# Narrow gate projections, decay rows by way of DRAM, full-row compressed values, and an earlier start in a two-block kernel

## The chip, the cores and the metric

One core of a Trainium2 chip runs the whole program. The metric is the device time of one execution in microseconds (us); the time given for a kernel is the median of its runs.

## What is computed

Two blocks follow each other on 512 latent rows of width 1024; the first also carries 256 context rows. In float32, cut to what matters here:

```python
for l in range(2):                                    # first block
    h  = rms_norm(x, g) * (1 + scale) + shift         # (shift, scale, gate) = silu(c) @ w_mod + b_mod
    hc = rms_norm(xc, g) * (1 + scale_c) + shift_c
    a*, b*, bg, c*, gm = split(h @ w_in)              # bg: 16 gate columns; same for hc
    y_a = diff_attention(...)                         # 4 heads
    y_b = mlstm(bq, bk, bv, bg)                       # 4 heads, both directions, decay matrix
                                                      # exp(b_t - b_s + i_s - m_t), masked
    y_c = neighbourhood_attention(cq, ck, cv)         # 8 heads of 64
    x, xc = merge(y_a, y_b, y_c, gm)
x = hybrid_ab(x) ; x = ffn(x)                         # second block
x = nsa(x) ; x = ffn(x)                               # 16 heads: compressed, selected and window
                                                      # values, each with a gate: 48 gate columns
```

## The kernel before

The activations stand transposed in SBUF: a chunk of 128 features by 512 latent and 256 context columns, split into a high and a low part (`hh`, `hl`). A projection of 128 output features takes a slot of weights: SP loads it as `raw` (`raw`, L327), ScalarE (ACT) casts the high part `whi` (L319), VectorE subtracts to get `wlo` (L320), and TensorE adds three products for each chunk of 128 inputs: `hh` with `whi`, `hl` with `whi`, `hh` with `wlo` (`proj`, L345; `tm_step` with tokens as the stationary side, L402). The slots lie in a ring of four, raw weights in three buffers, so SP loads some slots ahead.

The tile framework's scheduler sets the order of the instructions on each engine from the program text and the dependencies. The one exception is `start`, whose TensorE, VectorE and ScalarE instructions stand in the order of the text (L644).

The stages that the change touches:
- `start` (L611): layer 0. Latent and context columns are loaded, squared and summed on DVE, added over partitions by matmuls with a column of ones (`rstd`, L547), and spread as rows R (`rows`, L554). h is x times R, times scale, plus shift (`make_h`, L563, splits it); the products with R are DVE and GpSimd (POOL) instructions of their own (L650 to L673). Between them stand the units of the modulation, products of c with `w_mod` (`mod_products`, L486), whose row goes through ACT (L488) and two transposes (L746). The first value projection of the attention, `av`, runs alongside (L402). It takes all six row chunks for each pair of inputs. Layer 1's start (L1329) multiplies by R on DVE in the same way.
- The mLSTM gates, in `gates`: a projection with 16 columns (L345 with 128 x 16 weights), six transposes (L990), and a chain of small operations on rows that ends in Q (L1054), 48 columns, one for each direction, chunk and head.
- `mlstm`, once for each head: for each direction and chunk a column of Q is spread over the columns of a tile by a transpose of its broadcast (L1099), four to a bank; DVE adds the mask MK into the tile D (L1101) and ACT takes the exponential.
- `branch_c`, the neighbourhood attention: for each pair of heads and block of 128 queries two score tiles; a step later (`na_step`) their probabilities are transposed (L746), and a step after that `na_values` multiplies them with V (L1263), 64 columns for each head of the pair.
- NSA: `nsa_gates` (48 columns, four transposes L1819); `compress` makes VC, the compressed values; for each unit (group, query block, pair of heads) the probabilities are transposed four at a time (L746) and the unit before it is multiplied with V (L1972, 128 x 64). `nsa_values` is a generator, taken one group at a time between the transposes. Its first matmul is the compressed part with 64 rows of VC (L1968).

## Time and profile before

| | us |
|---|---|
| three runs | 3149.46, 3148.14, 3148.11 |
| median | 3148.14 |
| the profiled execution, its own time | 3147.98 |
| its span | 3146.2 |
| TensorE busy (in the span) | 3078.2 (98%) |
| VectorE busy | 1797.7 (57%) |
| ScalarE busy | 1257.6 (40%) |
| GpSimd busy | 300.9 (10%) |

The span is what the hardware profiler saw from the first instruction to the last, in one execution. An engine's busy time is the sum of its instructions' durations with overlaps counted once. TensorE's matmuls are pipelined: the next one starts before the one before has ended, so what a matmul costs is the distance from its start to the next start.

### The profile page before, as it was taken

How to read it: one execution, taken by the hardware profiler on the slowest of the kernel's cores; microseconds unless marked ns; L12 is line 12 of the kernel's file. 1: busy time of each engine (PE TensorE's matmuls, PEld its weight loads, DVE VectorE, ACT ScalarE, POOL GpSimd, SP SyncE). 2: the span in 40 equal slices, each digit the busy share in tenths (PEclk: the TensorE clock that was granted, in tenths of full speed). 3: DMA queues.
4: the chain of work that ended last, by engine and by line, in shares of the span. 5: the costliest groups of instructions: out<-in, count | busy, mean ns of one | idle time of the engine just before them, and what ended most of it. 6: DMA issues, size and time to landing. Idle time of an engine off the chain costs nothing.

```text
span 3146.2 us, 43890 instructions
## 1 busy us (share of the span) xinstructions
PE 3078.2 (98%) x17322; PEld 2572.0 (82%) x17322; DVE 1797.7 (57%) x3477; ACT 1257.6 (40%) x2382; POOL 300.9 (10%) x284
## 2 busy tenths in 40 slices
PE   7999999999999999999999999999999999999998
PEld 5888788888888888788888877788888788788887
DVE  6776256735574577346455477754433688644433
ACT  4553244325432356234344444332322267632221
POOL 1000000000015000000000400101100022101100
PEclk9999999999999999999999999999999999999999
DMA  6113211332235211311332533233223310022322
GB/s 225 41 34 135 71 60 48 127 115 72 84 138 205 87 49 48 111 54 61 110 104 88 161 100 102 67 101 101 94 94 104 99 41 28 28 94 94 101 92 69
DMA packets 86894, 285.96 MB, mean 91 GB/s; under 512 B 10400, under 2 KB 15264, under 8 KB 86304
## 3 DMA queue, kind: packets, MB, share of 16 engines
q1 hardware_dynamic: 68832, 237.60, 22.6%
q0 software_dynamic: 7424, 28.32, 2.5%
q10 hardware_dynamic: 10432, 17.24, 1.8%
q8 instruction: 136, 2.23, 0.3%
q14 instruction: 70, 0.57, 0.1%
HBM read 268.44 MB, written 14.68 MB: 90 GB/s over the span
## 4 chain that ended last, share of the span: by engine, by line
PE 88%; DVE 7%; issue 2%; ACT 2%; POOL 1%; DMA 0%; ACTq 0%; DVEq 0%; POOLq 0%
PE pj L345 57%; PE s L345 10%; PE s L746 4%; PE s L402 3%; PE s L741 2%; PE pj L402 2%; PE s L742 2%; PE s L1263 1%; PE pj L1972 1%; PE s L878 1%; PE s L1119 1%; DVE kl L737 1%; PE s L1145 1%; PE s L1138 1%; DVE kl L736 1%
## 5 line engine op out<-in xcount | busy, mean ns | idle before, releaser
L345 PE MATMUL pj<-hl,whi 128*128 128x512 f32 (+3 forms) x2696 | 939.5, 367 | 0.3 <-DVE hl L332 0.2
L345 PE MATMUL pj<-hh,whi 128*128 128x512 f32 (+3 forms) x2696 | 936.4, 369 | 2.6 <-ACT hh L331 0.8
L345 PE MATMUL pj<-hh,wlo 128*128 128x512 f32 (+3 forms) x2696 | 938.2, 367 | 0.0
L319 ACT CAST whi<-raw 128x1024 fp32r<-128x1024 f32 (+2 forms) x391 | 405.4, 1038 | 1088.8 <-PE pj L345 841.0
L320 DVE TENSOR_TENSOR wlo<-raw,whi 128x1024 fp32r<-128x1024 f32 (+2 forms) x391 | 488.1, 1249 | 443.4 <-ACT whi L319 434.4
L345 PEld LDWEIGHTS pj<-hh,whi 128*128 128x128 f32 (+2 forms) x2696 | 483.6, 187 | 92.7 <-issue 3.0
L345 PEld LDWEIGHTS pj<-hl,whi 128*128 128x128 f32 (+2 forms) x2696 | 483.0, 187 | 85.0 <-issue 1.9
L345 PEld LDWEIGHTS pj<-hh,wlo 128*128 128x128 f32 (+2 forms) x2696 | 482.9, 187 | 84.3 <-issue 1.7
L345 PE MATMUL pj<-uh,whi 128*128 128x512 f32 (+1 forms) x374 | 141.0, 377 | 0.0
L345 PE MATMUL pj<-ul,whi 128*128 128x512 f32 (+1 forms) x374 | 140.8, 376 | 0.0
L345 PE MATMUL pj<-uh,wlo 128*128 128x512 f32 (+1 forms) x374 | 140.8, 376 | 0.0
L741 PE MATMUL s<-kh,q 128*128 128x256 f32 (+1 forms) x320 | 101.2, 334 | 8.7 <-ACT kh L735 3.3
L700 ACT ACTIVATE th<-pj 128x512 f32<-128x512 f32 x72 | 37.3, 521 | 162.0 <-PE pj L345 150.3
L1715 DVE TENSOR_TENSOR a<-a,pj 128x512 f32<-128x512 f32 x44 | 30.3, 688 | 121.5 <-PE pj L345 121.5
L345 PE MATMUL s<-yh,whi 128*128 128x512 f32 (+1 forms) x288 | 98.7, 357 | 0.0
L345 PE MATMUL s<-yh,wlo 128*128 128x512 f32 (+1 forms) x288 | 98.0, 354 | 0.0
L345 PE MATMUL s<-yl,whi 128*128 128x512 f32 (+1 forms) x288 | 97.8, 354 | 0.0
L1713 POOL TENSOR_TENSOR a<-a,R 128x512 f32<-128x512 f32 x44 | 56.9, 1292 | 409.6 <-DVE a L1712 409.6
L1709 DVE TENSOR_TENSOR a<-pj,R 128x512 f32<-128x512 f32 x44 | 30.4, 691 | 113.5 <-PE pj L345 113.5
L742 PE MATMUL s<-kl,q 128*128 128x256 f32 (+1 forms) x320 | 92.7, 315 | 0.0
L345 PE MATMUL s<-hl,whi 128*128 128x512 f32 (+1 forms) x288 | 89.5, 347 | 0.0
L345 PE MATMUL s<-hh,wlo 128*128 128x512 f32 (+1 forms) x288 | 88.1, 345 | 0.0
(493 smaller groups left out, 4991.4 us busy)
## 6 DMA issues: line engine op xcount, KB each, us to landing
raw<-in_w SPq DMA_DIRECT2D x392, 512.0 KB, 3.4
mraw<-in_w SPq DMA_DIRECT2D x30, 512.0 KB, 4.9
bias<-in_bias ACTq DMA_DIRECT2D x16, 768.0 KB, 4.8
contrib<-cb POOLq DMA_DIRECT2D x16, 384.0 KB, 3.2
ld<-contrib POOLq DMA_DIRECT2D x16, 384.0 KB, 4.0
raw<-in_w SPq DMA_DIRECT2D x16, 384.0 KB, 2.9
contrib<-cb POOLq DMA_DIRECT2D x16, 256.0 KB, 2.6
ld<-contrib POOLq DMA_DIRECT2D x16, 256.0 KB, 3.1
```

Of the source, the lines that this page charges most:

```text
L319: nc.scalar.copy(hi[:, :width], raw[:, :width])
L320: nc.vector.tensor_sub(lo[:, :width], raw[:, :width], hi[:, :width].bitcast(F32))
L345: self.mm = self.nc.tensor.matmul(ps, wt[:, off + k * mcols:off + (k + 1) * mcols], acts[k][which][:, r], start=first and i == 0, stop=las ...
L402: self.nc.tensor.matmul(ps[c], self.h[k][a][:, P * c:P * c + P], b[:, w], start=k == 0 and pi == 0, stop=k == KD - 1 and pi == 2)
L700: self.nc.scalar.activation(th[:, r], p_, AF.Tanh, scale=0.5)
L736: nc.vector.tensor_sub(kl[a, c], r[a, c], kh[a, c].bitcast(F32))
L737: nc.vector.tensor_sub(kl[b, c], r[a, c], kh[a, c].bitcast(F32))
L741: self.nc.tensor.matmul(out, q[:, qs], kh[:, ks], start=True, stop=False)
L742: self.nc.tensor.matmul(out, q[:, qs], kl[:, ks], start=False, stop=True)
L746: self.nc.tensor.transpose(out[:, P * i:P * i + P], b, self.tab["id"])
L878: nc.tensor.matmul(po, at[:, P * i:P * i + P], V[:, k0 + i, P * h:P * h + P], start=i == 0, stop=i == nb - 1)
L1713: nc.gpsimd.tensor_mul(a, a, self.R)
```

## The change

- `narrow` replaces `proj` for the gate projections: high and low weights stand side by side as 32 (or 96) stationary columns, and two matmuls for each chunk, with `hh` and with `hl`, replace three. The two halves of the result are added by a matmul with a table of two stacked identities, which also transposes.
- Q is transposed once a layer, copied, and written by SP to `qrows` in DRAM; for each head SP loads its rows, broadcast to all partitions, into D, and DVE adds the mask in place.
- The neighbourhood values are multiplied two blocks at a time, with six buffers for the transposed probabilities.
- VC is padded with zeros to all 128 rows, one version for each pair of heads; `nsa_values` goes out in one piece ahead of the next unit's transposes.
- `start`: squares are added in pairs and the four sums by the matmuls with ones; the values' first slot is loaded ahead of the context; chunks of latent rows are multiplied for the first pair of inputs before the context's norm; the product with R is folded into `make_h`. Layer 1's start folds it too. Modulation units come in another order, and silu(c) moves into `start`.
- Smaller tiles of `compress` move to other buffers; the NSA gates are multiplied with R after their transposition.

The diff, cut:

```diff
+    def narrow(self, key, n, outs):
...
+        nc = self.nc
+        raw = self.raw(key)[:, :KD * n].rearrange("p (k f) -> p k f", k=KD)
+        w = self.t(self.ring, [P, SLOT], F32R, "whi", self.NRING)[:, :2 * n * KD].rearrange("p (k f) -> p k f", k=KD)
+        nc.scalar.copy(w[:, :, :n], raw)
+        nc.vector.tensor_sub(w[:, :, n:], raw, w[:, :, :n].bitcast(F32))
+        for ps, r in outs:
+            for k in range(KD):
+                for part in range(2):
+                    nc.tensor.matmul(ps, w[:, k, :], self.h[k][part][:, r], start=k == 0 and part == 0, stop=k == KD - 1 and part == 1)
...
-    def make_h(self, l, xs, js, part=None):
+    def make_h(self, l, xs, js, R, part=None, first=None):
...
-                nc.scalar.activation(hi[:, r], t[:, r], AF.Identity, bias=sh, scale=sc)
-                nc.vector.tensor_scalar(t[:, r], t[:, r], sc, sh, ALU.mult, ALU.add)
-            c = part[0] if part else slice(0, TT)
-            nc.vector.tensor_sub(lo[:, c], t[:, c], hi[:, c].bitcast(F32))
+                nc.vector.scalar_tensor_tensor(t[:, r], t[:, r], sc, R[:, r] if R.shape[-1] >= TT else R, ALU.mult, ALU.mult)
+                nc.scalar.activation(hi[:, r], t[:, r], AF.Identity, bias=sh)
+            if first:
+                first()
+            for r in part or both:
+                sh = mod[:, j, both.index(r):both.index(r) + 1]
+                nc.vector.scalar_tensor_tensor(lo[:, r], t[:, r], sh, hi[:, r].bitcast(F32), ALU.add, ALU.subtract)
...
-            units = [load(0)]
+            units = [load(0), load(1)]
+            av = [self.raw(("av", 0, 0))]
...
-            units.append(load(1))
-            ssq = self.t(sp, [P, TT], F32, "ssq")
+            units.append(load(2))
+            av.append(self.raw(("av", 0, 1)))
...
-                squares(lat)
-                rl = stats(lat)
-                squares(ctx)
+                rl = sums(squares(lat, range(4)), lat)
+                silu()
                 fin = self.mod_products(units[0], self.s1)
-                rows(lat, rl)
-                nc.vector.tensor_mul(xs[0][:, lat], rs[:, lat], xs[0][:, lat])
+                self.rows(rs, rl, 4)
+                slot = self.slot_hi(("av", 0, 0), av[0])
+                nc.scalar.copy(R[:, lat], rs)
                 fin()
-                rc = stats(ctx)
-                self.make_h(0, xs, (0,), (lat,))
-                slot = self.slot(("av", 0, 0))
                 fin = self.mod_products(units[1], self.s1)
-                rows(ctx, rc)
-                nc.vector.tensor_mul(xs[1][:, lat], R[:, lat], xs[1][:, lat])
+                self.make_h(0, xs, (0,), rs, (lat,), first=lambda: self.slot_lo(("av", 0, 0), *slot))
+                slot = slot[1:]
+                ps = self.tm_banks(NTC, True)
+                parts = self.tm_step("av", 0, 0, ps, 4, slot)
+                sq = squares(ctx, (0,))
                 fin()
-                self.make_h(0, xs, (1,), (lat,))
+                next(parts)
+                next(parts)
+                self.make_h(0, xs, (1,), R, (lat,))
+                fin = self.mod_products(units[2], self.s1)
+                sq += squares(ctx, (1, 2, 3))
+                next(parts)
+                fin()
+                units = [load(3)]
+                next(parts)
+                rc = sums(sq, ctx)
+                self.make_h(0, xs, (2,), R, (lat,))
+                slot = self.slot_hi(("av", 0, 1), av[1])
+                rows = self.s1()[:, :CTX]
+                self.rows(rows, rc, 2)
+                fin = self.mod_products(units[0], self.s1)
                 for j in range(2):
-                    nc.vector.tensor_mul(xs[j][:, ctx], R[:, ctx], xs[j][:, ctx])
-                    self.make_h(0, xs, (j,), (ctx,))
-                ps = self.tm_banks(NTC, True)
-                for s in range(4):
+                    self.make_h(0, xs, (j,), rows, (ctx,))
+                slot = self.slot_lo(("av", 0, 1), *slot)
+                nc.scalar.copy(R[:, ctx], rows)
+                self.make_h(0, xs, (2,), R, (ctx,))
+                next(parts)
+                fin()
+                self.make_h(0, xs, (3,), R)
+                for _ in parts:
+                    pass
+                for s in range(1, 4):
                     j = 2 * s + 2
-                    parts = self.tm_step("av", 0, s, ps, 4 * (s == 0), slot)
+                    parts = self.tm_step("av", 0, s, ps, 0, slot)
                     if s < 3:
                         units = [load(j + i) for i in range(2)]
                         next(parts)
                         fin = self.mod_products(units[0], self.s1)
                         slot = self.slot(("av", 0, s + 1))
-                        for i in range(2):
-                            (nc.vector, nc.gpsimd)[i].tensor_mul(xs[j + i], R, xs[j + i])
...
-        slot = self.slot(("bg", l))
-        outs = [(self.pj(SEQ, 16), slice(0, SEQ)), (self.pj(CTX, 16), slice(SEQ, TT))]
-        self.proj(slot, self.h, outs, mcols=16)
-        gs = self.t(sp, [16, TT], F32, "gs")
+        add = self.load(sp, "sum16")[0:32]
+        outs = [(self.pj(SEQ, 32), slice(0, SEQ)), (self.pj(CTX, 32), slice(SEQ, TT))]
+        self.narrow(("bg", l), 16, outs)
+        gs = self.t(sp, [32, TT], F32, "gs")
         for ps, r in outs:
-            nc.scalar.activation(gs[:, r], ps, AF.Identity, bias=self.par(("gate_b", l))[0:16])
+            nc.scalar.activation(gs[:, r], ps, AF.Identity, bias=self.par(("gate_b", l))[0:32])
...
         for c in range(NTC):
-            nc.tensor.transpose(pt[:, 16 * c:16 * c + 16], gs[:, P * c:P * c + P], self.tab["id"][0:16, 0:16])
+            nc.tensor.matmul(pt[:, 16 * c:16 * c + 16], gs[:, P * c:P * c + P], add, start=True, stop=True)
...
+        pq = self.s1()
+        nc.tensor.transpose(pq[0:48, :P], Q.rearrange("p d a h -> p (d a h)"), self.tab["id"])
+        qr = self.t(sp, [48, P], F32, "qr")
+        nc.vector.tensor_copy(qr, pq[0:48, :P])
+        nc.sync.dma_start(self.qrows[l], qr)
...
         D = [self.t(sp, [P, NTC, P], F32, f"D{d}", 1) for d in range(2)]
+        rows = qrows.rearrange("(d a h) t -> h d a t", d=2, a=6)
+        for d in range(2):
+            nc.sync.dma_start(D[d][:, :n, :], rows[h, d, :n].partition_broadcast(P))
         parts = []
         for cs in groups:
             parts.append([D[d][:, cs[0]:cs[-1] + 1, :] for d in range(2)])
             for d in range(2):
-                pe = self.s1()
-                for i, c in enumerate(cs):
-                    nc.tensor.transpose(ch(pe, i), Q[:, d, c, h:h + 1].to_broadcast([P, P]), self.tab["id"])
                 m = len(cs)
-                nc.vector.tensor_add(parts[-1][d], three(pe, m), MK[:, d, None, :].to_broadcast([P, m, P]))
+                nc.vector.tensor_add(parts[-1][d], parts[-1][d], MK[:, d, None, :].to_broadcast([P, m, P]))
...
-            pT = self.t(sp, [P, 512], F32, "pT", 4)
+            pT = self.t(sp, [P, 512], F32, "pT", 6)
             nc.scalar.copy(pT[:, :w], tp[:, :w])
             pTs.append(pT)
-        if ready:
-            self.na_values(*ready)
-        return pTs, *rest
-
-    def na_values(self, pTs, V, vt, out):
-
-        for x, j in enumerate(vt):
-            for i, pT in enumerate(pTs):
-                rows = slice(64 * i, 64 * i + 64)
-                self.nc.tensor.matmul(out[rows, :], V[:, j, rows], pT[:, P * x:P * x + P], start=x == 0, stop=x == len(vt) - 1)
+        if len(ready) == 2:
+            self.na_values(ready)
+        ready.append((pTs, *rest))
+
+    def na_values(self, ready):
+
+        for pTs, V, vt, out in ready:
+            for x, j in enumerate(vt):
+                for i, pT in enumerate(pTs):
+                    rows = slice(64 * i, 64 * i + 64)
+                    self.nc.tensor.matmul(out[rows, :], V[:, j, rows], pT[:, P * x:P * x + P], start=x == 0, stop=x == len(vt) - 1)
+        ready.clear()
...
-        VC = self.t(cp, [P, 4, P], F32, "VC")
+        VC = self.t(cp, [P, 2, 4, P], F32, "VC")
...
-            nc.vector.tensor_copy(VC[32 * x:32 * x + 32, :, r:r + 64], pt[0:32, :256].rearrange("p (g d) -> p g d", g=4))
+            nc.vector.tensor_copy(VC[32 * x:32 * x + 32, x // 2, :, r:r + 64], pt[0:32, :256].rearrange("p (g d) -> p g d", g=4))
...
             pr, cT, g, i, x, V, VC, y = unit
             blocks = [(k, r, j) for k in range(2) for j in range(i + 1) for r in range(2)]
             out = []
-        values = self.nsa_values(*ready) if ready else iter(())
+        if ready:
+            self.nsa_values(*ready)
         for b0 in range(0, len(blocks), 4):
             four = blocks[b0:b0 + 4]
...
-            next(values, None)
-        for _ in values:
-            pass
...
-        rows = slice(64 * x, 64 * x + 64)
         qs = slice(P * i, P * i + P)
-        nc.tensor.matmul(po, VC[rows, g, :], cT[rows, qs], start=True, stop=False)
+        nc.tensor.matmul(po, VC[:, x, g, :], cT[:, qs], start=True, stop=False)
...
-            if n == last:
-                nc.scalar.copy(y[:, qs], po)
-            yield
+        nc.scalar.copy(y[:, qs], po)
```

TensorE in the NSA stage, before: from a unit's window scores (L741, L742, with the parts `kwinh` and `kwinl` of the keys) over transposes (L746, with the identity `tab_id`) and values (L1968 compressed, L1972).

```order
L741 MATMUL s_3993_22565<-kwinh_21658,q_3822_21761 128x512
L742 MATMUL s_3993_22565<-kwinl_21659,q_3822_21761 128x512
L746 MATMUL s_3998_22584<-tab_id_77,pr_22441 128x128 x4
L1968 MATMUL pj_22591<-pcT_22130,VC_21326 128x128
L1972 MATMUL pj_22591<-pT_22482,V_21410 64x128 x4
L746 MATMUL s_4001_22597<-tab_id_77,pr_22441 128x128 x2
L746 MATMUL s_4001_22597<-tab_id_77,pr_22442 128x128 x2
L1972 MATMUL pj_22591<-pT_22495,V_21410 64x128 x4
L746 MATMUL s_4003_22608<-tab_id_77,pr_22442 128x128 x4
L1972 MATMUL pj_22591<-pT_22507,V_21410 64x128 x4
L741 MATMUL s_4009_22630<-kslch_21606,q_3844_21865 128x512
```

The same place with the change, where the scores are L799 and L800, transposes L804, the compressed values L2038 and the values L2042.

```order
L799 MATMUL s_3972_22456<-kwinh_21549,q_3801_21652 128x512
L800 MATMUL s_3972_22456<-kwinl_21550,q_3801_21652 128x512
L2038 MATMUL pj_22475<-pcT_22021,VC_21223 128x128
L2042 MATMUL pj_22475<-pT_22384,V_21301 64x128 x4
L2042 MATMUL pj_22475<-pT_22391,V_21301 64x128 x4
L2042 MATMUL pj_22475<-pT_22398,V_21301 64x128 x4
L804 MATMUL s_3978_22490<-tab_id_77,pr_22332 128x128 x4
L804 MATMUL s_3980_22497<-tab_id_77,pr_22332 128x128 x2
L804 MATMUL s_3980_22497<-tab_id_77,pr_22333 128x128 x2
L804 MATMUL s_3982_22504<-tab_id_77,pr_22333 128x128 x4
L799 MATMUL s_3988_22521<-kslch_21497,q_3823_21756 128x512
```

The values of a unit, which stood in three groups between the transposes, stand in one row of twelve ahead of them, behind the scores.

VectorE with the change, at the end of head 0 of layer 0's mLSTM: the outputs `hb` of head 0 (L1219, L1221), the additions of the mask to head 1's D (L1165), head 0's normalisation (L810, L812) and the next low weights (L328).

```order
L1221 SCALAR_TENSOR_TENSOR hb_3800<-nu_3993,dn_4001,hb_3800 128x128 x2
L1215 RECIPROCAL dn_4019<-dn_4019 128x2
L1165 TENSOR_TENSOR D_746_4317<-D_746_4317,MK_3477 128x512
L1219 TENSOR_SCALAR hb_3800<-nu_4013,dn_4019 128x128 x2
L1221 SCALAR_TENSOR_TENSOR hb_3800<-nu_4027,dn_4033,hb_3800 128x128 x2
L1165 TENSOR_TENSOR D_747_4318<-D_747_4318,MK_3477 128x512
L1165 TENSOR_TENSOR D_746_4317<-D_746_4317,MK_3477 128x256
L1165 TENSOR_TENSOR D_747_4318<-D_747_4318,MK_3477 128x256
L810 TENSOR_SCALAR on_r_4227<-ss_3801 128x6
L812 TENSOR_TENSOR hb_3800<-hb_3800,on_r_4227 128x768
L773 SCALAR_TENSOR_TENSOR sz_4099<-sz_4099,s_715_4049 128x512
L328 TENSOR_TENSOR wlo_4502<-raw_4499,whi_4501 128x1024
```

The additions, which before followed their own head's transposes (L1099) on TensorE, stand a head earlier, among the last operations of the head before.

TensorE with the change, at the end of the gates' chain in layer 0: the value projection (L422), the last small matmuls of the chain (L1096 to L1102), and the transpose of Q (L1119).

```order
L422 MATMUL pj_3487<-wlo_3621,hh_634 128x512
L1096 MATMUL s_599_3382<-tab_id_77,mr_3435 128x4 x6
L422 MATMUL pj_3487<-whi_3620,hl_635 128x512
L1101 MATMUL s_615_3445<-mt_3443,tab_id_77 128x48
L1102 MATMUL s_615_3445<-mt_3443,rev_3284 128x24
L1119 MATMUL s_622_3466<-tab_id_77,Q_3460 48x128
L422 MATMUL s_629_3488<-whi_3494,hh_246 128x512
```

The transpose is new there, straight behind the chain's last matmul.

## Rows read from the trace of the kernel before

**Rows 1.** The page's first and fourth parts: busy time and the chain that ended last.

```profile
PE 3078.2 (98%) x17322; PEld 2572.0 (82%) x17322; DVE 1797.7 (57%) x3477; ACT 1257.6 (40%) x2382; POOL 300.9 (10%) x284
...
PE 88%; DVE 7%; issue 2%; ACT 2%; POOL 1%; DMA 0%; ACTq 0%; DVEq 0%; POOLq 0%
```

**Rows 2.** Windows by stage: stretch, length, then busy us (instructions) of each engine, PE clock, DMA.

```profile
0.00:75.00 75.00, 52.23 (x434) 39.85 (x435) 45.97 (x90) 32.71 (x56) 8.59 (x9) 0.95 0.65 236
395.00:640.00 245.00, 244.88 (x1521) 217.92 (x1520) 156.09 (x378) 103.43 (x242) 7.54 (x8) 1.00 0.23 80
640.00:760.00 120.00, 120.00 (x755) 104.08 (x754) 49.90 (x98) 41.69 (x76) 2.16 (x4) 1.00 0.30 98
1370.00:1550.00 180.00, 179.98 (x983) 154.17 (x982) 109.18 (x252) 81.33 (x185) 6.27 (x8) 1.00 0.24 77
2535.00:2726.00 191.00, 186.65 (x1448) 148.85 (x1447) 154.44 (x531) 133.87 (x375) 45.94 (x38) 1.00 0.07 23
```

**Rows 3.** Timeline of PE, gate projection of layer 0: start, duration, engine, line, operation, tiles.

```profile
354.42 0.39 PE L345 MATMUL pj<-hh,whi 128*16 128x512 f32 x1
354.65 0.40 PE L345 MATMUL pj<-hl,whi 128*16 128x512 f32 x1
...
362.85 0.41 PE L990 MATMUL s<-tab_id,gs 16*128 16x16 f32 x4
```

**Rows 4.** Timelines of PE and DVE: the gates' chain, first and second head of layer 0.

```profile
383.50 0.32 PE L1043 MATMUL s<-mt,tab_id 128*128 128x48 f32 x2
383.65 0.37 PE L1044 MATMUL s<-mt,rev 128*128 128x24 f32 x2
383.86 0.48 PE L402 MATMUL s<-whi,hh 128*128 128x512 f32 x1
384.27 0.21 DVE L1054 TENSOR_TENSOR Q<-bt,mt 128x48 f32<-128x48 f32 x1
...
430.87 1.36 PE L1099 MATMUL s<-tab_id,Q 128*128 128x128 f32 x11
...
476.15 1.47 PE L1099 MATMUL s<-tab_id,Q 128*128 128x128 f32 x12
477.46 0.60 PE L746 MATMUL s<-tab_id,ack 128*128 128x128 f32 x4
```

**Rows 5.** The page's sixth part, DMA issues: tiles, queue, count, KB each, us to landing.

```profile
ld<-contrib POOLq DMA_DIRECT2D x16, 384.0 KB, 4.0
```

**Rows 6.** Timelines of PE: neighbourhood values (L1263) and NSA values.

```profile
779.33 0.66 PE L746 MATMUL s<-tab_id,p 128*128 128x128 f32 x4
779.92 0.87 PE L1263 MATMUL s<-pT,V 128*64 128x128 f32 x10
...
2609.25 0.48 PE L1968 MATMUL pj<-pcT,VC 64*128 64x128 f32 x2
2609.66 0.66 PE L1972 MATMUL pj<-pT,V 128*64 128x128 f32 x8
2610.25 0.66 PE L746 MATMUL s<-tab_id,pr 128*128 128x128 f32 x4
```

**Rows 7.** Timelines of PE and POOL: start of layer 0, and of layer 1 (last row).

```profile
12.74 0.58 PE L547 MATMUL s<-ones,ssq 128*128 128x1 f32 x2 [12.74 <-DVE ssq L539]
...
22.02 0.47 PE L402 MATMUL pj<-whi,hh 128*128 128x512 f32 x1
22.12 2.59 POOL L673 TENSOR_TENSOR x<-R,x 128x768 f32<-128x768 f32 x1 [1.56 <-ACT R L635]
...
34.04 0.69 PE L746 MATMUL s<-tab_id,row 128*128 128x128 f32 x2 [6.96 <-ACT row L488]
...
36.53 0.80 PE L402 MATMUL pj<-whi,hh 128*128 128x512 f32 x1
...
75.00 0.39 PE L345 MATMUL pj<-hh,whi 128*128 128x512 f32 x1
...
1078.31 0.73 PE L402 MATMUL pj<-whi,hl 128*128 128x512 f32 x2 [0.98 <-DVE hl L579]
```

123 lines of the change are left out of this document (74 added, 49 removed).

## The prediction

> **What bounds the kernel now.** The page's first part is read first: TensorE (PE) is busy 98% of the span and makes 88% of the chain that ended last, VectorE (DVE) 7% [rows 1]. So time falls where PE's own steps get fewer or shorter, and where one of its few waits goes. The windows come second, one for each stage that the change touches [rows 2]. In the mLSTM stages (395 to 640, 1370 to 1550) and in the neighbourhood stage (640 to 760) PE has at most 0.12 us of idle time and DVE is busy 42 to 64%: a PE step saved there is a step off the end. In the NSA scores and values (2535 to 2726) PE idles 4.35 us and DVE is busy 81%: a saved step counts only as far as DVE keeps up. In the start (0 to 75) PE is busy 52.23 us and idle 22.8 us: there the waits matter. Last come timelines of PE. Matmul durations overlap, so every price below is the distance from one start to the next, not a row's duration.
>
> **Gates.** The mLSTM gate projection is 48 matmuls a layer, from 354.42 to 362.85, 8.43 us [rows 3]. Two instead of three for each chunk take a third off: 2.8 us a layer, 5.6 for two. The stationary side grows from 16 to 32 columns; a step streams the same 512 or 256 rows of data, so I keep its price. The NSA gate is 24 matmuls of 512 columns, 8 go; at 0.23 us (354.42 to 354.65) 1.8 us. Against that, 16 transposes become 16 float32 matmuls, which show two passes each where a transpose shows one. The nearest small passes are L1043 and L1044, two each: 383.50 to 383.65 to 383.86 [rows 4], some 0.08 us a pass, so 16 more passes cost 1.3 us. Net **-6.1 us**, all on PE in full windows; bounds -7.4 (passes free) and -4.5 (passes twice as dear).
>
> **Decay rows.** Twelve transposes of one head take 476.15 to 477.46, 1.31 us or 0.109 each [rows 4]. There are 80 (12 in each head of layer 0, 8 in layer 1): -8.7 us. Added on PE are two transposes of Q, 0.2 us each with their change of shape, and a wait: the transpose's operand Q is written at 384.27 for 0.21 us, while PE is through with L1044 and starts the next matmul at 383.86 [rows 4]. If the transpose stands straight behind L1044, PE stands 0.6 us in each layer. Net **-7.2 us**.
> What was PE's becomes SP's: a 24 KB write to DRAM and two broadcast loads of 384 KB a head. The trace of before has no such round trip. Its nearest row is a load of 384 KB from DRAM, 4.0 us [rows 5]; one write and two loads, one after the other, are 12 us by it, and 24 if pieces of 512 bytes halve the rate. From 384.5 even 24 us end at 409, and the first head's decay is not used before 430.87 [rows 4]: hidden. Behind the loads on SP stand weight loads that could not start sooner. For the next head the tile D is the same buffer: its load waits for the last read by the head before, and DVE's additions to it stand ahead of that head's last normalisation (second order piece). DVE may thus stand 4 to 8 us, once for each of the 6 later heads. PE meanwhile has the bz projection, as many streamed columns as a gate slot of three parts (about 8.4 us), and then bq, whose parts were made before. I take 0; bounds 0 and 6 times 2 us.
>
> **Shape changes in the values.** A matmul of 128 rows by 64 columns between ones of 128 by 128 costs extra at both edges: four transposes alone are 4 x 0.109 = 0.44 us, but 0.59 between two groups of values (779.33 to 779.92), and eight values take 0.59 (2609.66 to 2610.25), of which the steps are 0.44 [rows 6]. So 0.15 us a change of shape. Counting changes in the two orders, the NSA stage goes from 164 to 82: 32 of them because VC fills all 128 rows (its two passes, 2609.25 to 2609.66, are 0.41 us where two of 128 columns are 0.22), 50 because a unit's values go out in one piece (first order piece). 82 x 0.15 = 12.3 us. DVE is 81% busy there and PE already waits on it; the last group of heads has no other work to fill with. I let 3 us be given back: **-9.3 us**, bounds -12.3 and 0. The neighbourhood stage loses 24 changes (three groups of values for a pair of heads instead of five, two instead of three in layer 1): **-3.6 us**, PE full there; bounds -3.6 and 0.
> The Trainium skill ("TensorEngine Tiling (Array Packing)", When to Use Tiling) speaks against the padding: for a contraction of 64 rows it wants 2x row tiling, two tiles working side by side, so filling up with zeros would forfeit a gain. By it the VC part of the sum would be 0 instead of 4.8 us. The trace does not bear it out so far: the 64-row passes stand alone and cost more than full ones.
>
> **Start.** PE's first matmul waits until 12.74 for the squares, the first value matmul starts at 22.02, a mod row's wait of 6.96 us ends at 34.04, values go on at 36.53 and branch a begins at 75.00 [rows 7]. After 36.53 PE is nearly full. The change (a) starts the values of chunks 0 and 1 with the latents alone, before the context's norm, (b) drops the separate multiplications by R, among them those on GpSimd (POOL) that begin at 22.12, one of 2.59 us, and with them most of the 6.96 us, and (c) makes 32 ones-matmuls 50. For (a) the context's chain of squares, norm and multiplication no longer stands ahead of 22.02; between 12.74 and 22.02 lie 9.3 us, and of these I take a good third, 3.4 us. For (b) 7.0. Against (c), 18 steps of two passes at 0.08 us [rows 4] are 2.9 us, half of them in time that is idle anyway, 1.4 us. **-9 us**; bounds -12 and 0, since every transfer of these 30 us shares the DMA engines, and the waits may only change their name. In layer 1's start the same folding takes one DVE pass out of the chain ahead of h, which ends in waits like that of 0.98 us at 1078.31 [rows 7]; I take one and a half of it, **-1.4 us**, bounds -2.5 and 0.
>
> **Sum.** 6.1 + 7.2 + 9.3 + 3.6 + 9 + 1.4 = 36.6 us. The profiled execution took 3147.98 us, of which 3146.2 are the span; it lies 0.16 under the median 3148.14, so the forecast of the profile and that of the median are the same: **3111 us**.
>
> **Rivals.**
> 1. *NSA is DVE's.* For: 154.44 of 191 us busy [rows 2], and what PE lacks there it waits for from DVE. Against: 4.35 us of idle time is little, so DVE is ahead mostly. If the whole stage keeps its length, 9.3 us less is gained: 3120 us. Chance 0.15.
> 2. *The start is the transfers'.* For: the DMA engines are 65% busy over the whole start [rows 2]. Against: the longest wait ends on ScalarE's copy of a row behind DVE and POOL work, not on a transfer. 3111 + 9 = 3120 us. Chance 0.15; both 1 and 2 together, 3129 us, 0.05.
> 3. *Full rows gain nothing.* The two 64-row halves would have worked together and padding undoes it: 4.8 us less, 3116 us. For it nothing in the rows, against it 0.41 us for two passes of 64 rows. Chance 0.05. The Trainium skill's rule above is this case.
> 4. *The DRAM round trip stops PE.* DVE stands at head h+1's decay with that head's bq, bk weight parts and head h's normalisation queued behind. PE then runs dry when the loads land later than bz's 8.4 us. The rows give some 4 us for one load and 8 for two in line, then four additions; if they come 10 us after the last read, nothing much is lost (6 x 2 us = 12 us: 3123). If they come at 16, behind weight loads in SP's queue, PE loses 8 us six times, 48 us, and the kernel is slower: 3111 + 48 = 3159 us. The point from which it decides is a loss of 6.1 us a head. For: single buffering of D, four large additions ahead of small work. Against: 36% of DVE and 77% of the DMA engines idle there [rows 2]. Chance 0.07: 0.03 over the point and slower, 0.04 near no change.
> The forecast itself keeps 0.53.
>
> **Numbers.** A difference of 0.2%, 6.3 us, is about what a measurement of this kernel can tell from no change. All cases but the fourth lie more than that under 3148.14: faster 0.93, within 0.2% 0.04, slower 0.03. The range runs from 3098 (all bounds on the good side: 36.6 + 1.3 + 3 + 3 + 1.1 = 45, and a few us for waits that go with the steps) to 3129, where rivals 1 and 2 together end.
>
> **What would show it.** Right: the gate projection 2 x 16 steps and 5.6 us long; no 128-column transposes of Q at each head and no PE idle time after bz; in 2535 to 2726 a stage some 9 us shorter with PE's waits on DVE up by about 3; values of the neighbourhood in groups of two blocks; first value matmul near 18.6 and branch a near 66. Wrong: DVE waiting over 8 us on the load of D with PE idle in the same place, or branch a still starting near 75, or the NSA stage still 190 us long.

## The result and the profile after

The changed kernel takes 3124.08 us (median of four runs, 3121.64 to 3128.25) against 3148.12 for the kernel before, run beside it: a ratio of 0.9924, interval [0.9907, 0.9942], 24 us faster. Run again later without an edit it took 3119.69 (3118.71 to 3121.26) against 3147.67, a ratio of 0.9912 [0.9899, 0.9926]: 28 us faster. So the median of one and the same kernel moved by 4.4 us between two sets of runs, while that of the kernel before moved by 0.5. The forecast was 3111, 37 us faster. Sign and place are as forecast; 9 to 13 us are missing. The trace below is that of the run of 3121.64 us; its span is 3119.9.

The page's parts 1 and 4 of the changed kernel, against [rows 1]:

```profile
PE 3057.6 (98%) x17256; PEld 2572.0 (82%) x17256; DVE 1782.3 (57%) x3472; ACT 1253.1 (40%) x2383; POOL 295.7 (9%) x281
...
PE 86%; DVE 7%; issue 2%; ACT 2%; POOL 1%; DMA 0%; ACTq 0%; DVEq 0%; POOLq 0%
```

TensorE lost 20.6 us of busy time and stays the bound. The windows of the same five stages, columns as in [rows 2]:

```profile
0.00:71.60 71.60, 60.91 (x470) 48.73 (x471) 36.81 (x83) 30.88 (x56) 2.35 (x6) 0.93 0.68 247
391.30:632.00 240.70, 240.64 (x1474) 213.30 (x1473) 154.29 (x374) 99.50 (x233) 7.53 (x8) 1.00 0.29 93
632.00:752.00 120.00, 120.00 (x757) 104.19 (x756) 49.74 (x98) 41.56 (x76) 2.16 (x4) 1.00 0.29 98
1355.50:1533.00 177.50, 177.50 (x955) 151.98 (x954) 108.04 (x251) 79.31 (x177) 6.27 (x8) 1.00 0.27 87
2515.70:2699.60 183.90, 175.37 (x1446) 149.72 (x1444) 152.02 (x531) 133.98 (x375) 46.42 (x38) 0.99 0.08 24
```

The mLSTM stages have next to no idle time (0.06 us and none), so every step saved there counts. In the NSA stage PE is busy 11.3 us less, but idles 8.53 us instead of 4.35. In the start PE idles 10.7 us instead of 22.8, yet the stage is only 3.4 us shorter, at a mean clock of 0.93 instead of 0.95.

All traces can be cut at the same projection matmuls (their order is the same in all kernels). The lengths of the stages in us, from one such start to the next:

| stage | before | change | again | early context |
|---|---|---|---|---|
| start of layer 0, up to branch a | 75.00 | 71.60 | 69.05 | 66.41 |
| branch a, mLSTM gates, its values | 330.73 | 329.93 | 329.94 | 329.86 |
| heads of the mLSTM, layer 0 | 184.72 | 180.03 | 180.08 | 180.04 |
| merge and neighbourhood, layer 0 | 305.82 | 303.61 | 303.45 | 303.56 |
| end of layer 0, start of layer 1 | 213.48 | 211.70 | 213.43 | 211.81 |
| branch a, gates, values, layer 1 | 262.88 | 261.66 | 261.67 | 261.45 |
| heads of the mLSTM, layer 1 | 123.35 | 119.94 | 119.90 | 119.88 |
| neighbourhood, layer 1 | 251.94 | 250.60 | 250.45 | 250.54 |
| end of layer 1, second block up to 2023.57 | 275.65 | 275.22 | 275.19 | 275.21 |
| from there to the last NSA values | 702.13 | 695.27 | 695.99 | 694.49 |
| from there to the last projection | 405.82 | 405.87 | 405.88 | 405.83 |

("Again" is the second trace of the changed kernel, "early context" an experiment below.) What fell short is the first row (3.4 and 5.95 us of 9) and the row that ends with the NSA values (6.9 and 6.1 of 10.8, the NSA gates included). The rows of gates, heads, neighbourhood and layer 1's start bring 15.5 us in the first trace of the 16.8 that the forecast has for them.

The start of the changed kernel, timeline of PE:

```profile
5.87 1.87 PE L572 MATMUL s<-ones,sq 128*128 128x1 f32 x8 [5.87 <-DVE sq L669]
8.97 5.28 PE L572 MATMUL s<-ones,sq 128*128 128x1 f32 x24 [1.24 <-DVE sq L669]
14.82 1.93 PE L508 MATMUL s<-raw,cl 128*32 128x128 f32 x32 [0.57 <-DVE cl L486]
...
21.21 0.50 PE L422 MATMUL pj<-whi,hh 128*128 128x512 f32 x1
...
24.50 1.08 PE L508 MATMUL s<-raw,cl 128*32 128x128 f32 x32
...
28.61 1.84 PE L572 MATMUL s<-ones,sq 128*128 128x1 f32 x16
31.93 0.69 PE L582 MATMUL s<-tab_id,rstd 128*128 128x128 f32 x2 [1.48 <-POOL rstd L577]
32.55 1.94 PE L508 MATMUL s<-raw,cl 128*32 128x128 f32 x32
35.38 0.80 PE L422 MATMUL s<-whi,hh 128*128 128x512 f32 x1 [0.90 <-ACT hh L605]
```

The first value matmul comes at 21.21, not at 18.6 (before: 22.02); in the second trace it comes at 19.56. The 24 values of the two latent chunks then run; at 28.61 the context's sums (L572) come, the power on GpSimd takes PE out for 1.48 us, and h of the context for another 0.90. The long wait of 6.96 us in [rows 7] is gone. But from about 31 the granted clock is halved, as it was before. Windows of the changed kernel, columns as in [rows 2], the clock third from the end; then the same of the kernel before:

```profile
30.00:35.00 5.00, 3.00 (x39) 2.04 (x38) 1.98 (x4) 2.11 (x4) 1.15 (x1) 0.61 0.36 124
35.00:40.00 5.00, 4.62 (x12) 3.64 (x13) 3.46 (x7) 1.60 (x4) 0.00 (x0) 0.50 0.56 201
40.00:45.00 5.00, 5.00 (x48) 3.80 (x47) 2.69 (x6) 1.59 (x4) 0.00 (x0) 0.87 0.01 3
```

```profile
30.00:35.00 5.00, 0.96 (x10) 0.61 (x14) 3.23 (x9) 2.40 (x4) 0.00 (x0) 0.67 0.26 104
35.00:40.00 5.00, 5.00 (x44) 3.91 (x37) 4.01 (x8) 1.68 (x3) 0.00 (x0) 0.64 0.58 182
```

At 0.50 the 32 matmuls of a modulation unit take 1.94 us (32.55) that take 1.08 at 24.50.

PE's waits in the NSA stage with its preparation (2450 to 2700; engine, tile and line, what it waited for, total us, times, longest):

```profile
PE s L804 <- DVE pc L1990: 1.9, 3, 0.6
PE s L799 <- ACT pT L2030: 1.8, 2, 1.2
PE s L1931 <- DMA pT<-in_w: 1.8, 1, 1.8
PE pj L2042 <- ACT pT L2030: 1.6, 3, 0.9
PE pj L353 <- ACT y L2043: 1.5, 1, 1.5
...
PE pj L2038 <- ACT y L2043: 0.8, 1, 0.8
```

In the trace before, the same stretch showed 4.5 us of waits, 3.4 of them on DVE's probabilities. Now 5.7 us end on ScalarE's copies (`pT`, `y`), and 1.8 on a load of 64 columns of weights that now goes into one of the buffers `pT`.

### The profile page after: what moved, and what is told of

The parts are those of the page before. It is cut to its first block, busy times and chain, and to the rows that moved or that the text cites. A ratio compares the mean times of both kernels' runs of the same rounds, so it can differ in the third digit from the quotient of the medians.

```text
span 3119.9 us, 43742 instructions
## 1 busy us (share of the span) xinstructions
PE 3057.6 (98%) x17256; PEld 2572.0 (82%) x17256; DVE 1782.3 (57%) x3472; ACT 1253.1 (40%) x2383; POOL 295.7 (9%) x281
## 4 chain that ended last, share of the span: by engine, by line
PE 86%; DVE 7%; issue 2%; ACT 2%; POOL 1%; DMA 0%; ACTq 0%; DVEq 0%; POOLq 0%
PE pj L353 57%; PE s L353 10%; PE s L422 3%; PE s L804 3%; PE s L799 2%; PE s L800 2%; PE pj L422 2%; PE s L1330 1%; PE pj L2042 1%; PE s L936 1%; PE s L1183 1%; DVE kl L795 1%; PE s L1209 1%; PE s L1202 1%; DVE kl L794 1%
## 5 line engine op out<-in xcount | busy, mean ns | idle before, releaser
L353 PE MATMUL pj<-hl,whi 128*128 128x512 f32 (+1 forms) x2656 | 928.4, 368 | 0.3 <-DVE hl L340 0.2
L353 PE MATMUL pj<-hh,whi 128*128 128x512 f32 (+1 forms) x2656 | 923.7, 370 | 4.1 <-ACT y L2043 1.5
L353 PE MATMUL pj<-hh,wlo 128*128 128x512 f32 (+1 forms) x2656 | 925.3, 368 | 0.0
L323 ACT CAST whi<-raw 128x1024 fp32r<-128x1024 f32 (+1 forms) x388 | 404.1, 1042 | 1072.2 <-PE pj L353 841.5
L328 DVE TENSOR_TENSOR wlo<-raw,whi 128x1024 fp32r<-128x1024 f32 (+1 forms) x388 | 487.7, 1258 | 441.4 <-ACT whi L323 431.9
L353 PEld LDWEIGHTS pj<-hh,whi 128*128 128x128 f32 x2656 | 479.3, 188 | 90.4 <-issue 3.3
L353 PEld LDWEIGHTS pj<-hl,whi 128*128 128x128 f32 x2656 | 479.3, 188 | 81.8 <-issue 1.8
L353 PEld LDWEIGHTS pj<-hh,wlo 128*128 128x128 f32 x2656 | 479.2, 188 | 80.7 <-issue 1.2
L799 PE MATMUL s<-kh,q 128*128 128x256 f32 (+1 forms) x320 | 100.3, 331 | 9.1 <-ACT kh L793 3.6
L800 PE MATMUL s<-kl,q 128*128 128x256 f32 (+1 forms) x320 | 91.7, 312 | 0.0
```

The costliest lines, as they stand in the source:

```text
L323: self.nc.scalar.copy(hi[:, :width], raw[:, :width])
L328: self.nc.vector.tensor_sub(lo[:, :width], raw[:, :width], hi[:, :width].bitcast(F32))
L353: self.mm = self.nc.tensor.matmul(ps, wt[:, off + k * mcols:off + (k + 1) * mcols], acts[k][which][:, r], start=first and i == 0, stop=las ...
L799: self.nc.tensor.matmul(out, q[:, qs], kh[:, ks], start=True, stop=False)
L800: self.nc.tensor.matmul(out, q[:, qs], kl[:, ks], start=False, stop=True)
```

## The experiments

All edits are to the changed kernel, and "slower" and "faster" are against its 3119.69 us. Only the start as before, the NSA values in groups and VC on 64 rows were run beside that figure. Since the kernel's own median moved by 4.4 us, a difference of a few us between the others and it decides nothing by itself: the stage lengths do, against its second trace.

**The change once more.** No edit.

> The changed kernel once more, nothing edited, for its spread and for a second trace. Four runs lay from 3121.64 to 3128.25 us where four of the kernel before lay within 2 us, and the mean granted clock of the changed kernel's runs went from 0.996 (shortest) to 0.993 (longest). Theory A: the length of the half-clock stretch in the start (about 33 to 41 us in the first trace) differs from run to run; then times again spread over 5 us or more, always longer at a lower mean clock, and a second trace shows the same span after 75 us as the first within 1 us. Theory B: the spread comes from the DMA round trips or from later stages; then two executions differ behind 75 us too.

3119.69 us, runs from 3118.71 to 3121.26, so the wide spread did not come back. The second trace has branch a at 69.05 and the clock back at full by 40 us (theory A's mechanism). But behind it the two traces differ by 2.2 us, more than the 1 us that theory A allowed (theory B): this one lost 1.7 us in layer 1's start (213.43 against 211.70 in the table). The place in this trace, and in the first one:

```profile
1055.00:1065.00 10.00, 8.59 (x98) 7.39 (x97) 4.93 (x20) 1.93 (x4) 1.35 (x1) 0.83 0.46 159
...
1055.81 1.50 PE L572 MATMUL s<-ones,ssq 128*128 128x1 f32 x12 [0.34 <-DVE ssq L561]
1057.23 1.11 PE L508 MATMUL pj<-mraw,cl 128*32 128x128 f32 x32
1058.13 1.92 PE L508 MATMUL pj<-raw,cl 128*32 128x128 f32 x32
```

```profile
1058.30 1.50 PE L572 MATMUL s<-ones,ssq 128*128 128x1 f32 x12 [0.34 <-DVE ssq L561]
1059.73 1.08 PE L508 MATMUL pj<-mraw,cl 128*32 128x128 f32 x32
1060.62 1.06 PE L508 MATMUL pj<-raw,cl 128*32 128x128 f32 x32
```

PE does the same in both, with the same short wait of 0.34 us; the second unit of 32 matmuls then takes 1.92 us in one execution and 1.06 in the other. So the clock falls in one execution and not in the next. That moves a run by 1.7 us at a time, and the stage table, not the median alone, has to decide small questions.

**The start as before.**

```diff
-                rl = sums(squares(lat, range(4)), lat)
...
+                squares(lat)
+                rl = stats(lat)
+                squares(ctx)
...
```

> The changed kernel with the start of layer 0 as before (separate multiplications by R, context's norm ahead of the first values, 6 ones-matmuls); all else as changed. By the first trace the new start is worth 3.4 us (branch a begins at 71.6 instead of 75.0), not the 9 of the prediction. Theory A: the new start is worth 3.4 us in its best runs and less or nothing in those with the longer half-clock stretch; then this kernel takes 3125 us (3124 to 3127), and its runs lie within 2 us of each other like those of before. Theory B: the start is worth the 9 us and something behind it gives 6 back in all versions; then 3130 us or more here. If the spread stays over 5 us, it has nothing to do with the start.

3128.04 us (3125.88 to 3129.23), 8.3 slower. Branch a begins at 74.67: the new start is worth 5.6 us against the second trace of the change, 3.1 against the first. The other 1.5 us between the traces lie in stages where this one shows the clock down (three places behind the start). The time is between A and B, and the spread stays at 3.4 us: not all of it comes from the start.

**NSA values in groups again.**

```diff
-        if ready:
-            self.nsa_values(*ready)
+        values = self.nsa_values(*ready) if ready else iter(())
...
+            next(values, None)
```

> The changed kernel with the NSA values of a unit again taken in groups between the next unit's transposes; VC still fills 128 rows. This puts 50 changes of shape back at 0.15 us, 7.5 us of TensorE steps. Theory A (whole units make ScalarE's copies come in bursts, and TensorE waits for them 5.6 us more than before): those waits go, so the kernel is 7.5 - 5.6 = about 2 us slower than the change. Rival B (TensorE's added waits have nothing to do with the grouping, VectorE being busy anyway): the full 7 us or more slower. Rival C (waits cost more than the steps save): faster than the change by 1 us or more.

3125.20 us, 5.5 slower; the stage is 700.87 us against 695.99, both with one drop of the clock in it: 4.9. PE's waits in it:

```profile
PE s L804 <- DVE pr L1875: 4.7, 10, 0.8
PE s L1931 <- DMA pT<-in_w: 1.8, 1, 1.8
```

The waits on ScalarE's copies do go (theory A), but 4.7 us on DVE's probabilities are there instead. Of the 7.5 us of steps, 2 to 2.6 are given back: the size lies between theory A's 2 us and rival B's 7.

**VC on 64 rows.**

```diff
-        nc.tensor.matmul(po, VC[:, x, g, :], cT[:, qs], start=True, stop=False)
+        nc.tensor.matmul(po, VC[64 * x:64 * x + 64, g, :], cT[64 * x:64 * x + 64, qs], start=True, stop=False)
...
```

> The changed kernel with VC on 64 rows again, values still in one piece. By the trace of before, two passes on 64 rows cost 0.41 us where the first trace of the change shows 0.31 to 0.33 for two on 128 rows with one change of shape; 32 units. Theory A (price of a change of shape 0.15 us): 32 x 0.15 = 4.8 us of steps more, of which waits may hide a third: 3 to 5 us slower than the change. Rival B (padding gains nothing, as row tiling would have it): the same time within 1 us, or faster.

3125.05 us, 5.4 slower; by the stage 700.12 against 695.99, 4.1, with one drop of the clock more in it. Between 2.4 and 4.1 us are the padding's. Rival B fell: padding gains.

**Gates by three products.**

```diff
-        self.narrow(("bg", l), 16, outs)
+        self.proj(slot, self.h, outs, mcols=16)
...
-        self.narrow(("ng", 3), 48, [(ps, slice(0, SEQ))])
+        self.proj(self.slot(("ng", 3)), self.h, [(ps, slice(0, SEQ))], mcols=48)
```

> The changed kernel with the gate projections as before: three products for each chunk, 16 (48) stationary columns, transposes. The sum of the prediction gave the narrow gates 6.1 us. In the trace of the change the mLSTM gates bring 2.5 and 2.8 us by the end of the projection, but the NSA gates' 1.8 us cannot be seen: TensorE waits 1.8 us there for a small weight load that now goes into a shared buffer. Theory A: gates are worth the steps, 5.6 + 1.8 - 1.3 = 6 us, and the new wait is hidden behind eight more NSA gate matmuls when they are back (they stand ahead of the waiting matmul), so up to 1.8 us of that returns: this kernel 4 to 6 us slower than the change (which took 3119.7 in the last call, 3124 in the first). Rival B: the added matmuls and the chain behind the projection eat the gain: under 2.5 us slower. One more or one less drop of the granted clock moves a run by some 1.7 us, so the trace by stages decides: in the mLSTM stage 2.8 us each.

3131.12 us (3129.77 to 3133.50), 11 slower, more than either said. The stages with the mLSTM gates take 331.74 and 264.22 us, 1.8 and 2.55 more than in the second trace of the change: 4.4 together, as the steps say. The NSA row is 702.68, 6.7 longer; the clock is halved in three places of it, 17.1 us together against 3.4, which at half clock costs some 6.8 us by itself, so they do not tell what the NSA gates are worth. That is left to the early small weights below.

**Decay on TensorE again.**

```diff
-                nc.vector.tensor_add(parts[-1][d], parts[-1][d], MK[:, d, None, :].to_broadcast([P, m, P]))
+                pe = self.s1()
+                for i, c in enumerate(cs):
+                    nc.tensor.transpose(ch(pe, i), Q[:, d, c, h:h + 1].to_broadcast([P, P]), self.tab["id"])
...
```

> The changed kernel with the decay's rows again spread by TensorE transposes for each head (no Q transpose, no DRAM write, no broadcast loads). Theory A: 80 transposes x 0.109 = 8.7 us return, 0.4 us of Q transposes and two waits of 0.6 us go: 7.1 us slower than the change, 1.2 to 1.3 us for each head of layer 0 and 0.8 to 0.9 for each of layer 1 in the trace. Rival B (the loads' round trip costs in DVE stalls, additions ahead of the normalisation, transfers beside the weights): under 4 us slower.

3128.11 us, 8.4 slower. The heads take 184.69 and 123.25 us, 4.6 and 3.35 more; the stages ahead of them 0.86 and 0.34 less, since the transposes of Q and their wait are gone: 6.8 us net. Theory A holds.

**Neighbourhood values one block at a time.**

```diff
-        if len(ready) == 2:
-            self.na_values(ready)
-        ready.append((pTs, *rest))
+        if ready:
+            self.na_values(*ready)
+        return pTs, *rest
```

> The changed kernel with the neighbourhood values one block at a time again (six buffers kept). Theory A: 24 changes of shape at 0.15 us: 3.6 us slower, 2.4 in layer 0 and 1.2 in layer 1. Rival B (the two-block order makes other waits, as in the NSA stage): within 1 us of the change. Rival C (later values delay what follows): faster.

3125.30 us, 5.6 slower; by the stages 306.09 and 252.14, 2.6 and 1.7 more: 4.3 us, with no drop of the clock in these rows of either trace. Theory A, a little above its 3.6; counted in the traces, 26 changes of shape come back, not 24.

**Context earlier.**

```diff
-                sq = squares(ctx, (0,))
+                sq = squares(ctx, range(4))
...
-                sq += squares(ctx, (1, 2, 3))
+                rc = sums(sq, ctx)
...
-                self.make_h(0, xs, (2,), R, (lat,))
-                slot = self.slot_hi(("av", 0, 1), av[1])
...
+                self.make_h(0, xs, (2,), R, (lat,))
+                slot = self.slot_hi(("av", 0, 1), av[1])
```

> The changed kernel with its start edited: all eight squares of the context ahead of h of chunk 1, their ones-matmuls ahead of chunk 1's values, the context's rows before the last three of these, h of both context chunks ahead of the third latent chunk. In the trace of the change TensorE idles 1.5 us for the power of the context's sums (30.45 to 31.93) and 0.9 us for h (34.5 to 35.4), and the granted clock is halved from about 31 to 38 or 41. Theory A (the context's norm stands in the values' way, and the clock falls because of these waits): branch a begins 3 to 6 us earlier than in the change (71.6 and 69.1 in two traces), and the kernel is 3 to 6 us faster. Rival B (the clock falls there whatever the order; the waits move elsewhere): less than 1.5 us. Rival C (the context's columns land too late, so the squares block ScalarE ahead of chunk 1): slower by 1 to 3 us.

3116.03 us (3115.32 to 3123.36), 3.7 faster. Timeline of PE and windows of its start:

```profile
24.46 1.95 PE L572 MATMUL s<-ones,sq 128*128 128x1 f32 x16
...
28.65 0.38 PE L582 MATMUL s<-tab_id,rstd 128*128 128x128 f32 x2
```

```profile
30.00:35.00 5.00, 4.22 (x43) 2.93 (x35) 3.00 (x6) 3.10 (x6) 0.00 (x0) 1.00 0.86 315
35.00:40.00 5.00, 4.24 (x45) 2.98 (x45) 3.92 (x9) 1.69 (x5) 0.00 (x0) 1.00 0.04 9
```

The power on GpSimd now lies beside chunk 1's values: the transposes of the context's rows (L582) wait for nothing, and the clock does not fall until the kernel's last 10 us. Branch a begins at 66.41, 8.6 us earlier than before the change and 2.6 to 5.2 earlier than in the change's two traces: theory A, at the lower end of its 3 to 6 us against the second of them. The rest of the 5.9 us that this trace gains on the second one is mostly luck: 3.1 of it lie in the two rows where only the other's clock fell.

The clock in the start goes with the order. In all nine traces with the start of before or of the change it is halved from some time between 30.5 and 33.3 us; in all five with the early context (this one and the four below) the window from 30 to 45 us shows 1.00. The order and the wait were changed together, so which of the two the clock goes by is not shown.

**Three more edits on top of it.** The compression's second weights and its table loaded at the head of that stage:

```diff
+        small = self.t(sp, [P, SEQ], F32, "pT", 6)
+        w2 = small[:, 2 * P:2 * P + 64]
+        nc.scalar.dma_start(w2, self.ap["w"][self.pl.slots[("w2",)][0], :, :64])
...
         for n in "kv":
```

> The early-context start (which took 3116.03 us, with no half-clock stretch before the end of its trace), and the compression's second weights and its rotary table loaded at the head of that stage instead of behind ScalarE's work in it. In every trace of the change TensorE waits 1.7 to 1.9 us for that load, with the rest of the NSA gates' matmuls queued behind. Theory A (that wait is what hides the 1.8 us of the narrow NSA gates): the wait goes, 1.8 us less: 3114 us, and between the stage's start and the values the kernel gains about 4.4 us on the one before, not 2.6. Rival B (the matmul waits for the chain of the gelu next, which ends at nearly the same time): under 0.7 us.

3116.25 us: no faster. The wait is gone, but the clock fell some 8 us behind that place in its trace, and twice in the second block's `hybrid_ab`. The second slot's kernel, below, has the same edit and kept its clock there. Windows of this one, then of that one:

```profile
2470.00:2480.00 10.00, 10.00 (x49) 8.05 (x49) 8.32 (x22) 3.12 (x6) 0.00 (x0) 0.83 0.17 56
```

```profile
2470.00:2480.00 10.00, 10.00 (x58) 7.84 (x57) 8.36 (x23) 3.13 (x6) 0.00 (x0) 1.00 0.24 79
```

PE is busy throughout in both, so a wait is not needed for the clock to fall. With the clock up the gain shows: between the projections that start at 2023.57 and 2540.5 before, the second slot's kernel gained 4.35 us on the trace of before, the two further kernels with this edit 4.4 each, the early-context kernel 2.54. Theory A, in the stage. The same place, timelines of PE: the second trace of the change, then the second slot's kernel.

```profile
2472.47 0.40 PE L375 MATMUL pj<-hl,whi 128*96 128x512 f32 x1
2474.67 0.43 PE L1931 MATMUL s<-pT,pT 64*64 64x124 f32 x4 [1.80 <-DMA pT<-in_w]
```

```profile
2468.68 0.40 PE L375 MATMUL pj<-hl,whi 128*96 128x512 f32 x1
2469.13 0.43 PE L1933 MATMUL s<-pT,pT 64*64 64x124 f32 x4
```

The load's issue, before and in the second trace of the change:

```profile
L1856 ACTq DMA_DIRECT2D w<-in_w x1: 742/742/742, 2438.3 to 2438.3; - x1
```

```profile
L1927 ACTq DMA_DIRECT2D pT<-in_w x1: 334/334/334, 2470.1 to 2470.1; - x1
```

Before, with a buffer of its own, it was issued 54 us ahead of its matmul (2492.46); in a buffer `pT`, 4.5 us ahead, and it takes 4.4 to land. With the edit it is issued at 2415.0.

The NSA values' result in another bank, besides:

```diff
-        po = self.pj(P)
+        po = self.s1()[:, :P]
```

> As the run before (early context, early small weights), and the NSA values' result in one of the six banks that scores and transposes use, instead of one of the two that the projections use. In the trace of the change a projection stands 1.5 us and a compressed product 0.8 us until ScalarE has copied the last result out of one of those two banks. Theory A: those two waits go and the others stay: 1.5 to 2.3 us faster than the run before. Rival B: the scores and transposes, which already wait 1.8 us for ScalarE's copies, wait longer for a bank: same or slower, by up to 3 us.

3116.64 us (3112.64 to 3119.66). The projection's wait of 1.5 us on `y` goes; the compressed product still waits 0.8 for it, now in its new bank, and scores wait for it too:

```profile
PE s L798 <- ACT y L2042: 2.3, 2, 1.2
PE s L2041 <- ACT pT L2029: 1.6, 2, 0.8
...
PE s L2037 <- ACT y L2042: 0.8, 1, 0.8
```

Inconclusive by its median; the runs lie further apart than before. The last run below settles it by the stage.

The second value slot split earlier, with early small weights and without the bank edit:

```diff
                 rc = sums(sq, ctx)
+                slot = self.slot_hi(("av", 0, 1), av[1])
```

> As the first run of this call (early context, early small weights), with the second value slot's split into high and low part moved ahead: the cast behind the context's sums, the difference ahead of h of the third chunk. In the early-context trace TensorE waits 0.8 us for that cast and 0.8 us for the difference, at 34 to 36 us. Theory A: both go: 1.5 us faster than the first run of this call. Rival B: the cast stands ahead of the context's h on ScalarE and the wait moves there: same within 0.7 us. Rival C: the clock falls again in the start: 3 us or more slower.

3115.74 us (3114.98 to 3116.58). Branch a begins at 65.86, 0.3 us before the first of these three, and 1.2 us of waits for h on ScalarE stand where the 1.6 for the slot were: rival B. Even the 0.3 is not the edit's for certain: the run with the bank edit, without this one, began branch a at 65.89.

**All together.**

> All edits together: early context, early small weights, early second slot, and the NSA values' result in one of the six banks. By the traces so far each execution of these kernels has none to three short half-clock stretches behind short idle times of TensorE, some 1.7 us each, at places that differ from run to run. Theory A: steps and waits add up: at full clock this kernel ends 2 us ahead of the one without the bank edit and 0.5 us ahead of the one without the slot edit, so 3114 us, with runs from 3112 to 3117 by the clock. Rival B: the bank edit brings as much half clock as it saves waits: 3116 us, no different from the three before it.

3114.92 us (3112.32 to 3118.40) against 3147.39: ratio 0.9901 [0.9884, 0.9917]. The shortest run is its profiled one: branch a at 65.92, the row that ends with the NSA values 691.90 us. The second slot's kernel, which lacks only the bank edit, has 693.65 there, and each of the two traces has one drop of the clock of the same length in that row: the bank edit is worth 1.75 us, inside theory A's 1.5 to 2.3 of that run. By the medians the kernel lies 32.5 us ahead of the one before and 4.8 ahead of the changed one (9.2 ahead of its first set of runs); the five versions with the early context cannot be told apart by their medians.

## Why the prediction was right, and where it was too large

The forecast of faster was right, because the two mLSTM stages and the neighbourhood stage have no idle time on PE and steps could be counted there. The time of 3111 us was not reached: the kernel came out where rivals 1 and 2 (3120 us each) put it, but by neither's mechanism.

- **Decay rows, -7.2** (7.1 by its own terms). Held: 6.8 net. The wait of Q's transpose, forecast at 0.6 us in each layer, is 0.61 in layer 0; in layer 1 none shows. The profile puts it down to the exponential `EM`, which ends at 379.52; Q itself is ready at 379.49. The round trip hides. Timelines and DMA issues of the change, against [rows 4, 5]:

```profile
378.66 0.37 PE L1102 MATMUL s<-mt,rev 128*128 128x24 f32 x2
379.63 0.27 PE L1119 MATMUL s<-tab_id,Q 128*48 128x128 f32 x1 [0.61 <-ACT EM L1125]
```

```profile
D<-qrows SPq DMA_DIRECT2D x8, 384.0 KB, 6.5
...
qrows<-qr SPq DMA_DIRECT2D x2, 24.0 KB, 2.2
```

  A load takes 6.5 us to land, not 4.0, inside the factor of two that was allowed. The fourth rival fell: DVE waits for D nine times in the two layers, 26.9 us together and 6.8 at most, and PE's idle time in the two stages is 0.06 us and none.
- **Neighbourhood, -3.6.** Held: 3.55 in the first trace's two rows, 4.3 by the undoing (26 changes of shape, where 24 were counted).
- **Gates, -6.1.** The mLSTM part (5.6 less 1.0 for the passes) held: 4.4 by the undoing; the projection of layer 0 runs from 351.32 to 356.82, 5.5 us. (The bound of -4.5 should read -4.8: 6.1 less 1.3.) The NSA part (1.8 less 0.3) did not show. The step that failed is one that the prediction did not cost: compression's small tiles moving to the buffers `pT`. It makes a load of weights late by 1.8 us, with PE's gate matmuls queued behind it. With the load early, the stage gains 1.8 us more (4.35 against 2.54).
- **Shape changes in NSA, -9.3.** The steps were right in the main: PE's busy time in the windows falls by 11.3 us of 12.3, and PE changes the shape of its stationary side 80 times instead of 160 there. The give-back was put at 3 us; idle time rose by 4.2 in these windows, and 5.7 of the 8.5 us end on ScalarE's copies, not on DVE as I argued. Undone one at a time, whole units are worth 4.9 us (7.5 were forecast, before any give-back) and full rows 2.4 to 4.1 (4.8). Rival 1 (the stage is DVE's) fell as it stood: the window is 7.1 us shorter. But a part is given back, mostly to another engine, and in groups PE does wait for DVE, 4.7 us.
- **Rival 3, full rows.** The Trainium skill ("TensorEngine Tiling (Array Packing)", When to Use Tiling) would keep 64 rows for a contraction of 64. Here 64 rows made the kernel 5.4 us slower by the median: the measurement decides against it where the 64-row matmul stands alone among full ones.
- **Start, -9.** Too large: 3.4 in the first trace, 5.95 in the second. Two terms were mis-sized. The 18 added ones-matmuls were put at 0.08 us a pass; the rows show 24 passes in 5.28 us, 0.22 each, in the first 15 us, and 16 in 1.84 us, 0.115, later. The trace before had that price, for [rows 7] shows only part of this row:

```profile
12.74 1.86 PE L547 MATMUL s<-ones,ssq 128*128 128x1 f32 x8 [12.74 <-DVE ssq L539]
```

  They took much of what (a) should have gained: the last sum of squares is ready at 11.51, PE is through with its passes at 14.25, and at 0.08 a pass it would have been at about 12.2 (an estimate from these rows). The first value matmul came 0.8 us earlier in the first trace and 2.5 in the second, not 3.4. And (b) counted all of the 6.96 us as won, though the context's sums, power and h make two new waits of 2.4 us at the place where the clock falls again. The early-context run shows that it was the order: 8.6 us, and with the same transfers, so rival 2 fell as well.
- **Layer 1's start, -1.4.** 1.8 where the clock stayed up, 0.05 where it fell.

The last part of the difference has no term in the prediction at all: the clock. Up to the last 12 us, it is halved for 10.2 us in the trace before and for 13.7 in each of the change's two, which makes some 1.7 us of the missing time in them. Behind the start the trace before shows one drop, those of the changed kernel and its variants none to four each.

## What to carry to other kernels

Where TensorE has no idle time, steps and changes of shape can be counted from the order: here the forecasts of 4.6, 7.2 and 3.6 us came out at 4.4, 6.8 and 3.6 to 4.3. Where it has waits, ask which in-order wait is next in line behind the one removed, and count every small load that moves to a shared buffer. Near 98% busy, undo one part at a time and compare stages, with the clock of each stage beside them: the median of one unedited kernel moved by 4.4 us between two sets of runs.

## What the runs showed of the chip

- The windows of the start read a clock of 1.00 from 0 on, while the same 32 matmuls of a modulation unit take 1.93 us at 14.82 and 1.94 at 18.16 that take 1.08 at 24.50 (and 1.94 again at 32.55, where the column shows the fall to half). By its steps TensorE starts at the lower of its levels, 1.2 GHz, which the column does not show; in the second trace of the change the step is back at 1.08 by 17.15. A price taken from later rows is about half of what it is there.
- At 98% busy the clock can fall or not at the same place of the same kernel, behind the same instructions and the same wait of 0.34 us (layer 1's start takes 211.7 or 213.4 us), and it can fall with PE busy for all 10 us of the window. No run here tells what decides it.
- Transfers to DRAM and back in 512-byte pieces cost TensorE nothing here: a write of 24 KB landed in 2.2 us, and 384 KB broadcast in 6.5, with no wait of PE in either mLSTM stage.
